# The first three tiles of a decoder layer side by side, and an account of the DMA wire in the planner

## The chip, the cores and the metric

The kernel runs on one core of one Trainium2 chip. The metric is the device time of one execution in microseconds (us); lower is better. TensorE multiplies matrices, VectorE (DVE) and ScalarE (ACT) work elementwise, GpSimd (POOL) fills and copies a little, and SP issues nearly all DMA transfers from one queue that it serves in order.

## The reference

One step of a decoder layer for a prompt of 256 tokens and 8 sequences of 8 new tokens: 320 rows of 2048 columns. One input projection feeds two token mixers (mLSTM, "ml", and HGRN2, "hg") and two merge gates; four more weight matrices follow.

```python
proj = jnp.einsum('btd,de->bte', x, w_in)
(ml_q, ml_k, ml_v, ml_i, ml_f, ml_o, hg_q, hg_f, hg_i, hg_g, gate_a, gate_b) = jnp.split(proj, offs, axis=-1)
h, C, n, m = _mlstm(q, k, v, ig, lf, C0, n0, m0)         # ig, lf from ml_i, ml_f
branch_a = norm(h) * jax.nn.sigmoid(ml_o)
o, S = _hgrn2(hq, jnp.log(f), 1.0 - f, hi, S0)           # f from hg_f
branch_b = rms(o) * jax.nn.silu(hg_g)
merged = jax.nn.sigmoid(gate_a) * (branch_a @ w_branch_a) + jax.nn.sigmoid(gate_b) * (branch_b @ w_branch_b)
x1 = _layernorm(DEEPNORM_ALPHA * x + merged @ w_out, ln1_g, ln1_b)
y = _layernorm(DEEPNORM_ALPHA * x1 + jnp.square(jax.nn.relu(x1 @ w_up)) @ w_down, ln2_g, ln2_b)
```

The outputs are y and the new states of both mixers. The mixers' states of the 8 sequences (C0: 4 heads, S0: 8 heads) are read from memory, updated and written back. All inputs are float32.

## The kernel before

**Main stream.** The six matrix products are cut into 304 tiles of 128 output columns (`tile_list`, `TILES`). A tile sums 16 k-steps of 128 rows into one PSUM bank. The tokens are the moving operand (320 columns), the weights the stationary one. Each float32 operand is split into a high half, rounded to the fast format fp32r (`xh`, `wh`), and the rest (`xl`, `wl`); a k-step is three products, high by high, high weight by low x, low weight by high x. So a tile is 48 products.

**Units.** Weights arrive as half tiles of 8 k-steps (`UNITS`, 512 KB each), in three raw buffers (`wr`, `RAW`). `prep` makes a unit's high half on ACT and its low half on VectorE, into one of three pairs of buffers (`wh`, `wl`, `HL`; five more from `bb` late in the kernel), and then plans the transfer of the unit three places on (`reload`) into the raw buffer just freed. The first six units are the first halves of tiles 0, 1, 2 and then their second halves (`FIRST` is 3).

**The start.** `start` issues the first transfers: unit 0 in three pieces from ACT's queue; x in pieces (k-steps 0, 1, 2 and 3, 4 to 7, 8 to 11, 12 to 15) from SP's queue, with units 1 and 2 between them; then the eight columns of the mLSTM gates (`wif`, in pieces of 32 bytes into a zeroed buffer `gw`), vectors and constants. Nine products of ones are issued on TensorE ahead of the real ones. `first` splits x and unit 0 piece by piece. After 24 k-steps, the first halves of tiles 0 to 2, `gates` multiplies x with `gw` in 16 small products of full float32; `rows` then computes the gate rows of the mLSTM (two products with `cst`, a chain of VectorE and ACT work, six transposes) and writes them to memory, from where each head reads them.

**Side work.** While the main stream runs, the evictions of the tiles and the mixers' work run beside it as Python generators ("chains"). A planner (`Sched`) writes the order of every engine by hand: it holds an assumed time for each engine and steps every chain that can go on, after each k-step of the main stream (`pump`). A chain's TensorE work is put into the order when its assumed operands are older than the assumed time of TensorE, and at most 0.9 us of it after each k-step. ACT and VectorE take a step that is assumed ready within 0.3 us if the engine is at most 0.9 us ahead. SP takes any that is ready within 0.3 us. A transfer is assumed landed a constant time after its issue (`+ 3200.0` for a unit, `+ 3500.0` for a part of C, `+ 4500.0` for S, `later(2500)` for an output). The times decide nothing but the order: on the chip, semaphores wait for what is really there, and every engine works off its order in sequence.

The input projection's side work lies in the first 850 us: 4 mLSTM heads, each with 16 parts of C loaded, used, updated and stored (256 KB each way, 14 buffers), then 8 HGRN2 heads with two groups of S each. From then on it is evictions and two layer norms; at the end a last part makes the prompt's new states and writes y.

Of the kernel before, what the change touches and what calls it, by code (L numbers as in the profile page):

```python
# [74 lines left out]
UNITS = [(i, half) for half in range(2) for i in range(FIRST)] + [(i, half) for i in range(FIRST, len(TILES)) for half in range(2)]  # L75
# [67 lines left out]
class Sched:  # L143
    PE_SIDE = 900.0

    def __init__(self):
        self.t = dict(pe=0.0, act=0.0, dve=0.0, pool=0.0, sp=0.0)
        self.chains = []
        self.pe_left = 0.0

# [7 lines left out]
    def use(self, eng, ready, cost):  # L158
        start = max(self.t[eng], ready)
        self.t[eng] = start + cost  # L160
        return start + cost

    def step(self, c, now):
# [27 lines left out]
        else:  # L191
# [18 lines left out]
            c.ready, c.eng, c.send = end, kind, end  # L210
        c.req = None
# [82 lines left out]
class Program:  # L294
# [43 lines left out]
    def dma(self, out, in_):  # L338
        self.nc.sync.dma_start(out, in_)  # L339

# [141 lines left out]
    def reload(self, u, at):  # L482
        t = yield ("sp", 620, lambda: self.dma(self.wr[:, u % self.RAW, :], self.d["wt"][u]), (at,))
        self.raw_at[u] = t + 3200.0

    def run_main(self):
        s = self.s
        todo = {}
        for n in range(len(TILES) * KT):
# [4 lines left out]
            if n == 0:  # L494
                self.first()
            elif n == 8 * FIRST:
                self.gates()
            if k == 0:
                self.before(i, t)
                s.until(lambda: self.mbank.free)  # L500
                self.mbank.free.sort(key=lambda x: x[0])
                at, b = self.mbank.free.pop(0)
                mh, ml, evs = self.moving(t)
                todo[i] = b, b[:, :mh.shape[2]], mh, ml, evs
                s.t["pe"] = max(s.t["pe"], at)
            b, o, mh, ml, evs = todo[i]
            if n < 8 * (FIRST + 1):
                s.t["pe"] = max(s.t["pe"], self.x_at[k], self.w_at[k] if u == 0 else 0.0)
# [20 lines left out]
        s.until(lambda: not s.chains)  # L529

# [79 lines left out]
    def start(self):  # L610
        nc, s, d = self.nc, self.s, self.d
        self.carve()
        P1 = self.Part(self.f1)
        xs, gw = P1.three(KT, TOK), P1.three(KT, 32)
# [6 lines left out]
        x = lambda lo, hi: self.dma(xs[:, lo:hi, :], d["xT"][:, lo:hi, :])  # L621
        for c in (slice(0, 256), slice(256, 512), slice(512, 1024)):
            nc.scalar.dma_start(self.wr[:, 0, c], d["wt"][0, :, c])
        nc.scalar.preload_act_table_set("natural_log_exp_and_others")
        x(0, 1)
        x(1, 2)
        x(2, 4)
        x(4, 8)
        self.dma(self.wr[:, 1, :], d["wt"][1])
        x(8, 12)  # L630
        self.dma(self.wr[:, 2, :], d["wt"][2])
        x(12, 16)
        nc.gpsimd.memset(gw, 0.0)
        self.dma(gw[:, :, 0:8], d["wif"])
        for u, at in ((1, 9000.0), (2, 12000.0)):
            self.raw_at[u] = at
        self.dma(self.vec, d["vec"])
        self.dma(self.cst, d["cst"])
# [9 lines left out]
        self.hl_free = [(0.0, (self.wh[:, i, :], self.wl[:, i, :])) for i in range(self.HL)]  # L648
        self.xs, self.gw = xs, gw
        for e in s.t:  # L650
            s.t[e] = 2000.0
        self.rows_ev, self.load_ev = Ev(), Ev()
# [20 lines left out]
    def first(self):  # L673

        s, v = self.s, self.nc.vector
        self.x_at, self.w_at = [0.0] * KT, [0.0] * 8
        hi, lo = self.hl_free.pop(0)[1]
        raw = self.wr[:, 0, :]
        f = lambda x: x.bitcast(F32)

# [7 lines left out]
        def x(a, b, at):  # L688
            c = slice(a, b)
            self.x_at[a:b] = [halves(self.xs[:, c, :], self.xh[:, c, :], self.xl[:, c, :], TOK * (b - a), at)] * (b - a)  # L690

        def w(a, b, at):
            c = slice(128 * a, 128 * b)
            self.w_at[a:b] = [halves(raw[:, c], hi[:, c], lo[:, c], 128 * (b - a), at)] * (b - a)

        x(0, 1, 3100.0)
        w(0, 2, 3500.0)
        x(1, 2, 3900.0)
# [1333 lines left out]
```

## Time and profile before

| | us |
|---|---|
| three timed runs | 2328.22, 2330.11, 2330.88 |
| their median | 2330.11 |
| the profiled execution's own time | 2327.19 |
| its span on the core | 2325.1 |
| TensorE busy in it | 2312.7 |
| VectorE, ACT busy | 1346.9, 1055.1 |

A timeline row gives start and length in us, engine, line of the kernel, operation, output<-inputs, shapes and a count; in brackets stands the idle time before it and what ended it. PE is TensorE, PEld its weight loads, SPq and ACTq are the engines' queues that issue transfers. A matmul's length overlaps the next one's, so the pace is the distance between starts. A windows row gives a stretch, its length, then each engine's busy time and number of instructions, the granted TensorE clock (PEclk, 1.00 is full), the busy share of the DMA engines and GB/s. A row of transfers gives count, size and the median time from issue to landing. A wait row gives who waited for whom: total us, times, longest.

### The profile page before, as it was taken

The numbers are of one execution on the slowest core, as the hardware profiler recorded it, in microseconds if no ns is written. First come the engines' busy times: TensorE is split into PE (matmuls) and PEld (weight loads), VectorE is DVE, ScalarE is ACT, GpSimd is POOL, SyncE is SP. The second block draws the span as 40 slices with busy tenths as digits, with TensorE's granted clock in tenths as the row PEclk, the third lists the DMA queues.
The fourth block names the chain that finished last, engine by engine and source line by source line (L and its number), as shares of the span: only waits on it lengthen the run. The fifth ranks groups of instructions, "written<-read, shape, count | busy, mean of one in ns | idle before, by whom it ended". The sixth has DMA issues, their size and how long they took to land.

```text
span 2325.1 us, 38931 instructions
## 1 busy us (share of the span) xinstructions
PE 2312.7 (99%) x15808; PEld 2270.0 (98%) x15808; DVE 1346.9 (58%) x2279; ACT 1055.1 (45%) x1685; POOL 11.5 (0%) x36
## 2 busy tenths in 40 slices
PE   9999999999999999999999999999999999999998
PEld 8999999999999999999999999999999999999997
DVE  5565566667676776555555767654444444444455
ACT  4444445455556665444433446542443343334333
POOL 0000000000000000000000000000000000000000
PEclk9999999999999999999999999999999999999999
DMA  7576858665555555555555644444444444444465
GB/s 247 195 258 204 291 187 281 224 215 173 196 181 188 182 185 172 177 174 172 176 171 174 215 166 154 147 152 146 154 146 154 146 154 147 153 148 152 149 221 183
DMA packets 145626, 424.91 MB, mean 183 GB/s; under 512 B 18468, under 2 KB 39972, under 8 KB 144424
## 3 DMA queue, kind: packets, MB, share of 16 engines
q1 hardware_dynamic: 143864, 415.63, 53.3%
q0 software_dynamic: 1152, 6.29, 0.8%
q8 instruction: 123, 2.02, 0.3%
q10 hardware_dynamic: 432, 0.52, 0.1%
q14 instruction: 55, 0.45, 0.1%
HBM read 371.48 MB, written 50.90 MB: 182 GB/s over the span
## 4 chain that ended last, share of the span: by engine, by line
PE 98%; ACT 1%; DMA 1%; SPq 0%; DVE 0%; issue 0%; ACTq 0%; DVEq 0%
PE bank L336 96%; DMA wr<-wt 1%; SPq L339 0%; ACT f3m L330 0%; PE bank L1158 0%; PE bank L929 0%; PE bank L1593 0%; PE bank L1431 0%; DVE f3m L1921 0%; ACT f L330 0%; PE bank L1485 0%; PE bank L1436 0%; PE bank L1002 0%; PE bank L976 0%; PE bank L1542 0%
## 5 line engine op out<-in xcount | busy, mean ns | idle before, releaser
L336 PE MATMUL bank<-xh,wh 128*128 128x320 f32 (+1 forms) x2432 | 785.6, 323 | 1.0 <-ACT xh L330 0.8
L475 DVE TENSOR_TENSOR wl<-wr,wh 128x1024 fp32r<-128x1024 f32 x431 | 528.0, 1225 | 423.1 <-ACT wh L330 419.0
L336 PE MATMUL bank<-xh,wl 128*128 128x320 f32 (+1 forms) x2432 | 754.5, 310 | 0.0
L336 PE MATMUL bank<-xl,wh 128*128 128x320 f32 (+1 forms) x2432 | 752.6, 309 | 1.3 <-DVE xl L685 1.3
L330 ACT ACTIVATE wh<-wr 128x1024 fp32r<-128x1024 f32 (+1 forms) x434 | 457.4, 1054 | 504.1 <-PE bank L336 486.1
L336 PEld LDWEIGHTS bank<-xh,wh 128*128 128x128 f32 x2432 | 459.0, 189 | 20.4 <-issue 15.0
L336 PEld LDWEIGHTS bank<-xl,wh 128*128 128x128 f32 x2432 | 459.4, 189 | 4.8 <-DVE xl L685 1.9
L336 PEld LDWEIGHTS bank<-xh,wl 128*128 128x128 f32 x2432 | 459.2, 189 | 0.1
L475 DVE TENSOR_TENSOR bb<-wr,bb 128x1024 fp32r<-128x1024 f32 x176 | 215.6, 1225 | 228.7 <-ACT bb L330 228.5
L330 ACT ACTIVATE bb<-wr 128x1024 fp32r<-128x1024 f32 x176 | 186.4, 1059 | 312.0 <-PE bank L336 292.8
L336 PE MATMUL bank<-xh,bb 128*128 128x320 f32 (+1 forms) x1280 | 285.4, 309 | 0.0
L336 PE MATMUL bank<-rxb,bb 128*128 128x320 f32 x1208 | 276.3, 309 | 0.0
L336 PE MATMUL bank<-ra,wh 128*128 128x320 f32 x988 | 265.9, 309 | 0.0
L336 PE MATMUL bank<-ra,bb 128*128 128x320 f32 x1096 | 264.3, 309 | 0.7 <-DVE ra L1623 0.7
L336 PEld LDWEIGHTS bank<-xh,bb 128*128 128x128 f32 x1280 | 215.0, 188 | 0.0
L336 PEld LDWEIGHTS bank<-rxb,bb 128*128 128x128 f32 x1208 | 204.5, 188 | 0.2
L336 PE MATMUL bank<-xl,bb 128*128 128x320 f32 (+1 forms) x640 | 197.7, 309 | 0.0
L336 PEld LDWEIGHTS bank<-ra,bb 128*128 128x128 f32 x1096 | 187.1, 188 | 1.2 <-DVE ra L1623 0.9
L336 PEld LDWEIGHTS bank<-ra,wh 128*128 128x128 f32 x988 | 176.3, 188 | 0.0
L336 PE MATMUL bank<-rxb,wh 128*128 128x320 f32 x548 | 169.0, 308 | 0.0
L336 PE MATMUL bank<-rxb,wl 128*128 128x320 f32 x548 | 169.0, 308 | 0.0
L336 PEld LDWEIGHTS bank<-xl,bb 128*128 128x128 f32 x640 | 120.4, 188 | 0.3 <-DVE xl L1846 0.3
(261 smaller groups left out, 2213.7 us busy)
## 6 DMA issues: line engine op xcount, KB each, us to landing
wr<-wt SPq DMA_DIRECT2D x607, 512.0 KB, 3.3
rx<-C SPq DMA_DIRECT2D x34, 256.0 KB, 5.2
Cs<-rx SPq DMA_DIRECT2D x34, 256.0 KB, 5.0
f<-C SPq DMA_DIRECT2D x30, 256.0 KB, 4.7
Cs<-f SPq DMA_DIRECT2D x30, 256.0 KB, 4.6
vD<-ra SPq DMA_DIRECT2D x4, 1024.0 KB, 9.0
f<-S SPq DMA_DIRECT2D x8, 512.0 KB, 6.1
f3h<-S SPq DMA_DIRECT2D x8, 512.0 KB, 6.6
```

Source lines behind the costliest of these rows:

```text
L330: return self.nc.scalar.activation(out, in_, func, **kw)
L336: self.nc.tensor.matmul(*a, **kw)
L475: self.V().tensor_tensor(lo, raw, hi.bitcast(F32), ALU.subtract)
```

## The change

**The first three tiles** leave `UNITS`. A new input `first` holds, for every k-step, x (320 columns) and the three tiles' weights (3 x 128) side by side (`STEP`, 704 columns). `start` loads it into `f1` and `f3`: k-step 0 as weights from ACT's queue and x from SP's, then k-steps 1, 2, 3 alone and the others in pairs from SP's. Then come the gates' columns, now contiguous and spread into `gw` by a POOL copy, vectors, and the first three units (of tiles 3 and 4). `lead` takes the place of `first`: it splits each k-step's x and weights on ACT and VectorE and issues the nine products of the k-step into three banks, by kind of product over the three tiles in the first four k-steps and tile by tile from then on. The weights' halves use `wh` and `wl` as eight slots of 384 columns. After the last k-step the evictions of the three tiles are put into the order, then the preparation of two units, then the gates' products.

**The planner** keeps a time for the DMA wire. A transfer is assumed to begin 1.5 us after its issue or when the wire is free, to take its bytes at 380 bytes per ns, and to land 0.6 us later; this landing replaces the constants. SP takes a step only if it is at most 0.9 us ahead, and not before the eighth transfer back is assumed landed. This holds for all transfers planned after the start.

```diff
-UNITS = [(i, half) for half in range(2) for i in range(FIRST)] + [(i, half) for i in range(FIRST, len(TILES)) for half in range(2)]
+UNITS = [(i, half) for i in range(FIRST, len(TILES)) for half in range(2)]
+STEP = TOK + 128 * FIRST
...
+    def transfer(self, at, size):
+        self.wire = max(at + 1500.0, self.wire) + size / 380.0
+        self.lands.append(self.wire + 600.0)
...
+            elif kind == "sp":
+                if r > now + 300 or self.t[kind] > now + 900:
+                    return False
+                r = max(r, self.lands[-8])
             elif r > now + 300:
                 return False
             end = self.use(kind, r, cost)
             fn()
             c.ready, c.eng, c.send = end, kind, end
+            if kind == "sp":
+                c.send = self.lands[-1]
...
     def dma(self, out, in_):
         self.nc.sync.dma_start(out, in_)
+        self.s.transfer(self.s.t["sp"], 4 * math.prod(out.shape))
...
-        self.raw_at[u] = t + 3200.0
+        self.raw_at[u] = t
...
-        for c in (slice(0, 256), slice(256, 512), slice(512, 1024)):
-            nc.scalar.dma_start(self.wr[:, 0, c], d["wt"][0, :, c])
+        first = d["first"]
+        nc.scalar.dma_start(self.xw[0][:, TOK:STEP], first[:, 0, TOK:STEP])
         nc.scalar.preload_act_table_set("natural_log_exp_and_others")
...
+        self.dma(self.xw[0][:, 0:TOK], first[:, 0, 0:TOK])
+        for lo, hi in ((1, 2), (2, 3), (3, 4), (4, 6), (6, 8), (8, 10), (10, 12)):
+            self.dma(raw[0][:, lo:hi, :], first[:, lo:hi, :])
+        for lo in (0, 2):
+            self.dma(raw[1][:, lo:lo + 2, :], first[:, 12 + lo:14 + lo, :])
         nc.gpsimd.memset(gw, 0.0)
-        self.dma(gw[:, :, 0:8], d["wif"])
+        self.dma(wif, d["wif"])
+        nc.gpsimd.tensor_copy(gw[:, :, 0:8], wif.rearrange("p (k n) -> p k n", n=8))
         self.dma(self.vec, d["vec"])
+        for u in range(self.RAW):
+            self.dma(self.wr[:, u, :], d["wt"][u])
+            self.raw_at[u] = 19000.0 + 1500.0 * u
...
+        pe = 4700.0
+        for k in range(KT):
+            at = 3400.0 + 950.0 * k
+            c = slice(384 * (k % 8), 384 * (k % 8) + 384)
+            xh, xl = self.xh[:, k, :], self.xl[:, k, :]
+            halves(self.xw[k][:, 0:TOK], xh, xl, TOK, at)
+            pe = max(pe, halves(self.xw[k][:, TOK:STEP], wh[:, c], wl[:, c], 384, at))
+            hi, lo = wh[:, c], wl[:, c]
+            jobs = [(i, w, x) for i in range(FIRST) for w, x in ((hi, xh), (hi, xl), (lo, xh))]
+            if k < 4:
+                jobs = [jobs[3 * i + j] for j in range(3) for i in range(FIRST)]
+            for n, (i, w, x) in enumerate(jobs):
+                self.mm(bank[i][:, :TOK], w[:, 128 * i:128 * i + 128], x, start=k == 0 and w is hi and x is xh, stop=k == KT - 1 and w is lo)
+                if k == KT - 1 and n % 3 == 2:
+                    s.t["pe"] = pe + 147.0 * (n + 1)
+                    s.spawn(self.evac(TILES[i], bank[i]), 0)
+            pe += 147.0 * 3 * FIRST
+            for i, last in enumerate((10, 13, 15)):
+                if k == last:
+                    self.hl_free.append((pe, (self.wh[:, i, :], self.wl[:, i, :])))
+        s.t["pe"] = pe + 300.0
+        s.pump(s.t["pe"])
+        s.t["pe"] = pe
         self.prep(True)
-        x(8, 12, 11000.0)
         self.prep(True)
-        x(12, 16, 13500.0)
...
-            self.mm(b[32 * x:32 * x + 32, :TOK], self.gw[:, k, :], self.xs[:, k, :], start=k < 4, stop=k >= KT - 4)
-        s.t["pe"] += 2500.0
+            self.mm(b[32 * x:32 * x + 32, :TOK], self.gw[:, k, :], self.xw[k][:, 0:TOK], start=k < 4, stop=k >= KT - 4)
+        s.t["pe"] += 2200.0
         s.spawn(self.rows(b), 1)
         s.spawn(self.lb(), 2)
+        s.pump(s.t["pe"])
...
-        m["bc_"].t = t + 3000.0
+        m["bc_"].t = t
...
-    def later(self, dt):
+    def later(self):
         e = Ev()
-        e.t = self.s.t["sp"] + dt
+        e.t = self.s.lands[-1]
         return e
...
-            m["parts"][n].t = t + 3500.0
+            m["parts"][n].t = t
...
-        m["ld"].t = t
+        m["ld"].t = self.s.t["sp"]
         m["sat"] = Ev()
-        m["sat"].t = t + 4500.0
+        m["sat"].t = t
```

More of the change, by code (lines that the diff above doesn't have):

```diff
@@ L529, in run_main, with take @@
         s.until(lambda: not s.chains)
+    def take(self):
+        s = self.s
+        s.until(lambda: self.mbank.free)
+        self.mbank.free.sort(key=lambda x: x[0])
+        at, b = self.mbank.free.pop(0)
+        s.t["pe"] = max(s.t["pe"], at)
+        return b
     def give(self, u):
@@ L814, in rows @@
         self.scr = scr
[L815 removed]
+        self.scr_at = t0
     def m_start(self, h):
```

99 lines of the change are left out of this document (35 added, 64 removed).

## The prediction

> **What bounds the kernel now.** I read the page first: busy shares, then the chain that ended last.
>
> ```profile
> span 2325.1 us, 38931 instructions
> PE 2312.7 (99%) x15808; PEld 2270.0 (98%) x15808; DVE 1346.9 (58%) x2279; ACT 1055.1 (45%) x1685; POOL 11.5 (0%) x36
> PE 98%; ACT 1%; DMA 1%; SPq 0%; DVE 0%; issue 0%; ACTq 0%; DVEq 0%
> ```
>
> TensorE is the bound, and a change can win only where it waits or runs slow. The windows view, cut at the places that matter, says where that is.
>
> ```profile
> core 0: us, PE busy (x) PEld busy (x) DVE busy (x) ACT busy (x) POOL busy (x), PEclk, DMA share, GB/s
> 4.99:8.41 3.42, 2.11 (x8) 1.15 (x7) 2.26 (x5) 2.31 (x6) 0.00 (x0) 1.00 1.03 406
> 8.41:15.23 6.82, 5.80 (x20) 5.40 (x21) 5.86 (x6) 5.30 (x5) 0.00 (x0) 0.50 0.96 314
> 15.23:21.98 6.75, 6.75 (x48) 6.56 (x46) 1.62 (x2) 1.19 (x2) 0.40 (x1) 1.00 0.94 314
> 21.98:24.27 2.29, 2.29 (x34) 0.94 (x33) 1.54 (x2) 1.68 (x3) 0.00 (x0) 1.00 0.13 48
> 24.27:36.87 12.60, 12.42 (x81) 10.89 (x77) 6.86 (x15) 5.29 (x11) 0.20 (x1) 1.00 0.51 166
> 36.87:100.00 63.13, 63.13 (x439) 60.85 (x438) 38.49 (x73) 28.58 (x44) 0.00 (x0) 1.00 0.68 236
> 100.00:850.00 750.00, 750.00 (x5236) 718.46 (x5235) 495.26 (x1111) 397.14 (x795) 4.66 (x13) 1.00 0.63 212
> 850.00:2298.00 1448.00, 1447.34 (x9858) 1446.33 (x9857) 776.84 (x1026) 596.49 (x790) 4.38 (x8) 1.00 0.49 163
> 2298.00:2325.00 27.00, 18.91 (x84) 15.47 (x83) 18.17 (x44) 15.47 (x31) 0.00 (x0) 0.89 0.60 222
> ```
>
> From 36.87 to 2298 us the idle time is 0.66 us in all: the second half of the change, which touches those 2261 us, finds nothing to win there in waits. In 850:2298, 9858 products took 1448 us, so one product at full clock is 0.1469 us. The loss is at the start, and the timeline shows its parts.
>
> ```profile
> 0.73 1.39 ACTq L623 DMA_DIRECT2D wr<-wt  x3
> 0.74 1.82 SPq L339 DMA_DIRECT2D f<-xT  x4
> 0.99 4.17 PE L336 MATMUL bank<-ones 128*128 128x128 f32 x18 [0.99 <-POOL ones L616]
> 4.59 0.47 ACT L330 ACTIVATE xh<-f 128x320 fp32r<-128x320 f32 x1 [1.16 <-DMA f<-xT]
> 4.97 0.40 ACT L330 ACTIVATE wh<-wr 128x256 fp32r<-128x256 f32 x1
> 5.09 0.49 DVE L685 TENSOR_TENSOR xl<-f,xh 128x320 fp32r<-128x320 f32 x1 [5.09 <-ACT xh L330]
> 5.27 0.47 ACT L330 ACTIVATE xh<-f 128x320 fp32r<-128x320 f32 x1
> 5.42 0.41 PE L336 MATMUL bank<-xh,wh 128*128 128x320 f32 x1 [0.26 <-ACT wh L330]
> 5.50 0.42 DVE L685 TENSOR_TENSOR wl<-wr,wh 128x256 fp32r<-128x256 f32 x1
> 5.84 0.49 DVE L685 TENSOR_TENSOR xl<-f,xh 128x320 fp32r<-128x320 f32 x1
> 6.63 0.32 PE L336 MATMUL bank<-xh,wl 128*128 128x320 f32 x1
> 7.74 0.41 PE L336 MATMUL bank<-xh,wh 128*128 128x320 f32 x1 [0.79 <-ACT xh L330]
> 8.59 0.63 PE L336 MATMUL bank<-xl,wh 128*128 128x320 f32 x1 [0.45 <-DVE xl L685]
> 11.40 0.64 PE L336 MATMUL bank<-xl,wh 128*128 128x320 f32 x1 [0.84 <-DVE xl L685]
> 21.98 2.36 PE L336 MATMUL bank<-f 128*32 128x320 f32 x32
> 27.37 0.70 PE L336 MATMUL bank<-f,cst 128*4 128x320 f32 x2 [0.18 <-ACT f L330]
> 36.87 0.30 PE L336 MATMUL bank<-xh,wh 128*128 128x320 f32 x1
> ```
>
> The first half units of tiles 0 to 2 are 72 products: 5.42 to 21.98, 16.56 us against 72 x 0.1469 = 10.58. The 5.98 us are waits for pieces of x (7.74, 8.59, 11.40) and a granted clock of 0.50 from 8.41 to 15.23, which the idle stretches brought on. Then come the gates' products (21.98), the second halves, and at 36.87 the first product of tile 3.
>
> **The change, part by part.** (a) *Loads.* A k-step now brings x (160 KB) and three weight pieces (192 KB) at once, and feeds nine products, 1.32 us, where a k-step of x fed three, 0.44 us. What was hungry is the first pass: it needed all of x (2.5 MB) and half the weights within 10.6 us. Now the pass takes 144 x 0.1469 = 21.15 us and needs 5.77 MB. The wire, one number per us from 0:
>
> ```profile
> GB/s 0 22 204 251 338 390 420 394 417 430 398 424 405 155 66 117 364 298 287 365 410 303 94 16 29 299 287 221 254 385 99 0 33 254 238 0 0 90 352 94
> ```
>
> From 5 to 13 us it moves 410 GB/s, so 0.36 MB every 0.88 us: ahead of TensorE. x's first 160 KB were on the wire together with the ACT queue's 128 KB (0.3 MB moved at about 3.4 us) and were used at 4.59, 1.2 us later. By the same sums k-step 1 (0.72 MB moved) is usable at 5.9, 2 at 6.9, 3 at 7.8, 4 at 9.6, 6 at 11.3, 14 at 18.3.
>
> (b) *Splitting.* ACT's starts are 0.38 us apart after 320 columns (4.59, 4.97) and 0.30 after 256 (4.97, 5.27), so about 0.46 after 384: 0.84 a k-step. VectorE: 0.41 (5.09, 5.50) and 0.34 (5.50, 5.84), so 0.48 and 0.89. Both stay below TensorE's 1.32, so TensorE becomes the pace. The first weight piece is wider by 128 columns: its ACT copy takes about 0.54 instead of 0.40, so the first product starts near 5.56 instead of 5.42, 0.14 later. TensorE then asks for k-step 1 at about 6.9 (split from 5.9, high half ready 6.8), 2 at 8.3, 3 at 9.6, 4 at 10.9, 6 at 13.6: all there. The first six products of before start about 0.24 apart (5.42 to 6.63); for the same unsteadiness I allow 0.3. The pass ends at 5.56 + 21.15 + 0.3 = 27.0.
>
> (c) *Evictions, then preparation, then gates.* On ACT the three evictions now stand ahead of the high halves of tile 3's first unit, so these wait for the end of the pass. From like rows:
>
> ```profile
> 37.07 0.44 ACT L330 ACTIVATE f<-bank 128x320 f32<-128x320 f32 x1 [1.78 <-PE bank L336]
> 37.40 0.45 ACT L330 ACTIVATE f<-f 4x320 f32<-4x320 f32 x1
> ```
>
> and the page's groups of the same copy and subtraction:
>
> ```profile
> L330 ACT ACTIVATE wh<-wr 128x1024 fp32r<-128x1024 f32 (+1 forms) x434 | 457.4, 1054 | 504.1 <-PE bank L336 486.1
> L475 DVE TENSOR_TENSOR wl<-wr,wh 128x1024 fp32r<-128x1024 f32 x431 | 528.0, 1225 | 423.1 <-ACT wh L330 419.0
> ```
>
> An eviction occupies ACT 0.33 us; the last starts 0.2 after the pass's end, the unit's high half follows at +0.5 and lasts 1.05, its low half 1.23, so it is there at +2.85. The gates' 32 products cover 2.39 of that (2.29, and an allowance of 0.1 for the change of operands), the next two products 0.4: 0.1 is left as a wait. If the gates' cover were gone, it would be 2.4. The second unit is ready at about +4.1 and wanted at +5.9. The next reload can start at +2.9 and is wanted three units (10.6 us) later.
>
> (d) *POOL and the queues.* The gates' columns now arrive in one contiguous transfer and are spread by one POOL copy (at most the 0.40 us POOL is busy in 15.23:21.98, for twice the columns); it waits for a transfer behind 5.8 MB, about 18 us, and POOL's memsets queue behind it, first wanted after 27. SP moves the first three units (1.5 MB, 3.8 us at 410 GB/s) behind x: there at about 22.5, wanted at 27. ACT issues one transfer instead of three (1.39 us at 0.73); its gain is covered by the 1.16 us in which ACT waits for x. All nothing.
>
> (e) *Row products.* 24.27:36.87 holds 72 products (10.58) and 2.02 of row products with their 0.18 wait (27.37 is the first pair). They come after tile 3's start now, at the same cost.
>
> (f) *The account of the wire* changes only in which order work is issued. It replaces constants after the issue: a unit's reload 3.2 becomes 1.5 + 1.38 + 0.6 = 3.48 on an idle wire, a C part 3.5 becomes 2.79, and more behind other transfers. Measured from the issue:
>
> ```profile
> wr<-wt SPq DMA_DIRECT2D x607, 512.0 KB, 3.3
> rx<-C SPq DMA_DIRECT2D x34, 256.0 KB, 5.2
> ```
>
> and SP's own waits:
>
> ```profile
> SPq L339 <- DVE wl L475: 879.5, 307, 15.0
> ```
>
> For C the account errs toward too early by 0.71 more than the constant did. If each of the 8 C groups and 8 S groups then stood 0.71 too early in TensorE's order, that is 11.4 us lost; at the other end nothing, since TensorE shows no wait for them. I take 0, the value that 100:850 shows under the old constants. Side products may also fall into other places. A return from a transpose to the main stream:
>
> ```profile
> 45.24 0.39 PE L336 MATMUL bank<-xh,wh 128*128 128x320 f32 x1
> 45.47 0.31 PE L336 MATMUL bank<-xl,wh 128*128 128x320 f32 x1
> ```
>
> 0.23 instead of 0.147, so 0.08 a return; 15 places more or fewer are 1.2 us, either sign. I take 0.
>
> *Sum.* Before: tile 3 at 36.87, less the row products 2.02: 34.85. After: 27.0 + 2.39 + 0.1 = 29.5. The gain is 5.3 us, all at the start. Of the profiled execution, 2327.19 us (span 2325.1), that leaves 2321.9. The three timed runs are 2328.22 to 2330.88, median 2330.11, 2.9 above the profiled one; by the median it is 2324.8. I see only the start's clock stretches as a cause for such a spread (the granted clock changed after 3.42 and again after 6.82, twice 3.41; 3.41 us at half clock cost 1.7), and a pass without idle time should meet fewer, so I go between: 2323.5.
>
> *A rule against a row.* In 4.99:8.41 TensorE was busy 2.11 of 3.42 us, and the clock halved after it; in the first half of 8.41:15.23 it stood idle 0.84 us before 11.40 and the clock stayed low. So partly busy stretches cost the clock here. The Trainium skill (TensorE: Matmul & The Clock Gate, What's actually happening) has the array go to half rate after at least one idle window of about 3.4 us, and back after a busy one. By that no stretch after the change would be slowed; the trace does not bear the first half out, and the sum by the row is the first rival.
>
> **The rivals.** *1. The clock still halves.* After the change the stretch 4.99:8.41 has about 2.7 to 3.0 busy us of 3.42: between the 2.11 that lost the clock and a full one. One such stretch costs 1.7: 2325.2; two, 2326.9. Against it: x and weights are there, so a slowed TensorE is full and recovers. 0.20.
>
> *2. Late weights: slower.* SP now refuses a transfer when it is more than 0.9 us ahead, reloads among them, and an assumed landing moves by up to eight transfers. If in the crowded loads of C a reload falls behind and its unit is late, TensorE waits a unit's ACT and VectorE time, 1.05 + 1.23 = 2.3 us. One in each of the 8 C groups: 18.4, so 2342. From the fifth it is slower by over 0.2% (5.3 + 4.7 = 10.0). For it: SP spends 879.5 us waiting for buffers of the units, and what stands behind waits too. Against: three buffers give 10.6 us, the turn needs 1.05 + 1.23 + 3.3 = 5.6, and the wire is 63% busy. 0.10.
>
> *3. The gain is given back* in side products (1.2), some early C groups (0.71 each) and the end: 2298:2325 is bound by ACT, VectorE and output transfers, whose order the account may change. Some 4 us: 2327.5. 0.12.
>
> *4. The pieces do not overlap.* Sixteen k-steps in eleven transfers, each taking its whole time from issue to landing, at the least the 3.85 us from 0.74 to 4.59: 42 us, so the pass ends some 16 us later than I say: 2339. The wire's row, 390 to 430 GB/s with pieces of 128 to 640 KB, speaks against it. 0.02. The Trainium skill (DMA: Bandwidth & Descriptors, Measured) advises transfers of 1 MiB or more for 75% of peak and would count against pieces of 352 KB; this trace does not agree while several are queued.
>
> **How the numbers follow.** Forecast 0.56, with its own range 2320 to 2326.5 (1.2 for side products, 2 for the clock). A measurement here tells about 0.2%, 4.7 us: faster means below 2325.4, slower above 2334.8. Faster: most of the forecast and a third of rival 1, 0.58. Same: the rest of rival 1, rival 3 and the forecast's edge, 0.30. Slower: rivals 2 and 4, 0.12. The range runs from 2319 (the profiled execution's sum less 1.2 and one clock stretch) to 2330 (rival 3 with a clock stretch), and leaves out rivals 2 and 4 and a little below.
>
> **What would show it.** First product near 5.6; no wait over 0.3 us on TensorE until the gates' products near 27; clock 1.00 from 5 us on (rival 1: a 0.50 stretch); tile 3 near 29.5. ACT and VectorE a step ahead throughout the pass. No idle time on TensorE from 37 to 2298 us and no wait on a wr transfer (rival 2). The end still 27 us long. I am wrong if x or weights arrive later than the wire's row says, if C or S products wait, or if the number of returns changes by dozens.

## The result

Before and after were timed in turn on one chip, seven runs each. Before has a median of 2329.77 us (2328.22 to 2332.29), after 2321.28 us (2320.65 to 2321.49). The ratio is 0.9962, with a 95% interval of 0.9951 to 0.9974: 8.5 us less. The profiled execution of after took 2321.41 us (span 2319.6), 5.8 us less than that of before. The forecast was 2321.9 for the profiled execution and 2323.5 for the median.

The page of after begins:

```profile
span 2319.6 us, 38982 instructions
PE 2309.1 (100%) x15808; PEld 2267.0 (98%) x15808; DVE 1351.6 (58%) x2297; ACT 1059.5 (46%) x1703; POOL 11.9 (1%) x37
PE 98%; ACT 1%; DVE 0%; DMA 0%; issue 0%; SPq 0%; ACTq 0%; DVEq 0%
```

Still 15808 products and nearly the same busy time; the 1% of the chain that lay on DMA is gone. The stretches of after, in the same columns as those of before:

```profile
4.86:8.41 3.55, 3.22 (x22) 2.95 (x22) 2.25 (x6) 2.12 (x5) 0.00 (x0) 1.00 1.02 367
8.41:15.23 6.82, 6.82 (x47) 6.56 (x46) 6.08 (x15) 5.77 (x15) 0.00 (x0) 1.00 1.01 411
...
29.42:872.69 843.27, 843.27 (x5874) 807.63 (x5871) 560.30 (x1224) 446.23 (x871) 4.68 (x13) 1.00 0.64 213
```

Between 8.41 and 15.23, where before ran 20 products at half clock, 47 products run at full clock. The timeline of after shows the places that the prediction spoke of:

```profile
3.93 0.47 ACT L342 ACTIVATE xh<-f 128x320 fp32r<-128x320 f32 x1 [1.47 <-DMA f<-first]
4.86 0.71 PE L348 MATMUL bank<-xh,wh 128*128 128x320 f32 x3
7.17 0.47 ACT L342 ACTIVATE xh<-f 128x320 fp32r<-128x320 f32 x1 [1.33 <-DMA f<-first]
8.10 0.71 PE L348 MATMUL bank<-xh,wh 128*128 128x320 f32 x3 [0.33 <-ACT wh L342]
18.83 0.42 POOL L646 COPY f<-f 128x128 f32<-128x128 f32 x1 [17.42 <-DMA f<-wif]
27.13 1.82 PE L348 MATMUL bank<-f,f 128*32 128x320 f32 x24
27.57 2.00 ACT L342 ACTIVATE wh<-wr 128x1024 fp32r<-128x1024 f32 x2
29.42 0.42 PE L348 MATMUL bank<-xh,wh 128*128 128x320 f32 x1
29.68 0.31 PE L348 MATMUL bank<-xl,wh 128*128 128x320 f32 x1
29.93 0.41 PE L348 MATMUL bank<-xh,wl 128*128 128x320 f32 x1
```

The first product starts at 4.86, the gates' at 27.13, tile 3 at 29.42; in before these stood at 5.42, 21.98 and 36.87, with 2.02 us of row products ahead of tile 3 that after has behind it. Of TensorE's waits after the start only those for a k-step's weights (0.33 us, at 8.10) and for the last part of the kernel (0.7 us) are left.

To compare all kernels I cut the span at two products of the main stream, counted in the traces: the first of tile 3 and the first of tile 103, 4800 main products later, behind the mixers' last side work. Before's row for the stretch between them:

```profile
36.87:878.46 841.59, 841.59 (x5868) 807.75 (x5867) 553.09 (x1211) 442.27 (x865) 4.66 (x13) 1.00 0.63 213
```

That is 841.59 us against 843.27, and 843.27 less the 2.02 us of row products is 841.25: nothing is lost or won there, between these two executions. (One group of C takes 0.6 us longer in this execution of after than in e_after's below.) The rest of the span is 1446.63 us in before and 1446.94 in after. So the 5.5 us by which the spans differ are the start: 36.87 - 2.02 - 29.42 = 5.43.

### The profile page after: what moved, and what is told of

It is laid out like the page before. It is cut to its first block, busy times and chain, and to the rows that moved or that the text cites. A ratio compares the mean times of both kernels' runs of the same rounds, so it can differ in the third digit from the quotient of the medians.

```text
span 2319.6 us, 38982 instructions
## 1 busy us (share of the span) xinstructions
PE 2309.1 (100%) x15808; PEld 2267.0 (98%) x15808; DVE 1351.6 (58%) x2297; ACT 1059.5 (46%) x1703; POOL 11.9 (1%) x37
## 3 DMA queue, kind: packets, MB, share of 16 engines
q8 instruction: 123, 2.02, 0.4%
## 4 chain that ended last, share of the span: by engine, by line
PE 98%; ACT 1%; DVE 0%; DMA 0%; issue 0%; SPq 0%; ACTq 0%; DVEq 0%
PE bank L348 97%; ACT f3m L342 0%; DMA f<-first 0%; PE bank L1610 0%; PE bank L946 0%; PE bank L1175 0%; PE bank L1448 0%; DVE f3m L1938 0%; ACT f L342 0%; PE bank L1453 0%; PE bank L1019 0%; PE bank L1502 0%; PE bank L993 0%; PE bank L1559 0%; ACT oC L342 0%
## 5 line engine op out<-in xcount | busy, mean ns | idle before, releaser
L488 DVE TENSOR_TENSOR wl<-wr,wh 128x1024 fp32r<-128x1024 f32 x426 | 522.0, 1225 | 399.6 <-ACT wh L342 395.9
L342 ACT ACTIVATE wh<-wr 128x1024 fp32r<-128x1024 f32 x426 | 451.0, 1059 | 498.1 <-PE bank L348 478.2
```

Source lines behind the costliest of these rows:

```text
L342: return self.nc.scalar.activation(out, in_, func, **kw)
L488: self.V().tensor_tensor(lo, raw, hi.bitcast(F32), ALU.subtract)
```

## The experiments

In the profiled executions of all kernels (us):

| | tile 3 starts | tile 3 to tile 103 | tile 103 to the end | execution |
|---|---|---|---|---|
| before | 36.87 | 841.59 | 1446.63 | 2327.19 |
| e_before | 38.89 | 842.54 | 1446.53 | 2329.75 |
| e_fill | 35.98 | 841.99 | 1446.55 | 2326.47 |
| e_account | 37.84 | 841.51 | 1446.47 | 2327.93 |
| e_lead | 29.56 | 850.51 | 1446.22 | 2328.46 |
| e_lead_c | 29.66 | 847.76 | 1446.71 | 2326.23 |
| e_lead_s | 29.03 | 852.91 | 1446.76 | 2330.56 |
| e_queue | 29.33 | 844.85 | 1446.29 | 2322.70 |
| e_landings | 29.84 | 842.87 | 1447.06 | 2321.56 |
| e_after | 29.58 | 842.79 | 1446.82 | 2320.95 |
| after | 29.42 | 843.27 | 1446.94 | 2321.41 |
| e_pieces | 29.84 | 842.86 | 1446.59 | 2321.36 |
| e_two_queues | 29.48 | 842.67 | 1447.08 | 2321.01 |
| e_late_evict | 29.52 | 842.60 | 1446.92 | 2320.84 |

The last column differs from the start times and stretches by the 2 us around the span. Each ratio below is against before, timed in the same batch on the same chip. Rows with the new start hold 2.02 us of row products in the second column that the others do not.

### What the old start costs: e_before and e_fill

The prediction's median rested on a guess: that before's executions differ by stretches of halved clock at the start. e_before is before, unchanged. e_fill keeps TensorE busy in the first pass with products of ones into a bank that the gates' products overwrite later:

```diff
             kk = slice(128 * (k % 8), 128 * (k % 8) + 128)
+            self.fill({2: 4}.get(n, 0))
             self.mm(o, hi[:, kk], mh[:, k, :], start=k == 0, stop=False)
+            self.fill({2: 2, 4: 8}.get(n, 0))
             self.mm(o, hi[:, kk], ml[:, k, :], start=False, stop=False)
...
+    def fill(self, count):
+        for _ in range(count):
+            self.mm(self.gbank[:, 0:128], self.ones, self.ones, start=True, stop=True)
```

> The kernel before, unchanged, to see the granted clock of each timed execution. Theory A (the 3 us by which the profiled execution lies below the median of the kernel before are half-clock stretches at the start, which fall differently from run to run): the mean clock differs from execution to execution, lower where the time is longer, and each 1.7 us of time goes with about 0.0015 in the mean clock (3.41 us at half clock out of 2325); times spread over 3 us or more. Rival B (the spread has nothing to do with the clock): the mean clock is 0.997 in all of them.

Measured: median 2329.16 us (2327.60 to 2332.01, 11 runs), ratio 1.0001 (0.9993 to 1.0010). Its profile caught a slower execution than the one in the prediction: 2.0 us more at the start, 1.0 us more in the mixers' stretch. At the start k-steps 2 and 3 of x were late. From the timeline of before, then from the timeline and the windows of e_before:

```profile
6.94 0.74 ACT L330 ACTIVATE xh<-f 128x640 fp32r<-128x640 f32 x1 [0.90 <-DMA f<-xT]
```

```profile
8.53 0.74 ACT L330 ACTIVATE xh<-f 128x640 fp32r<-128x640 f32 x1 [2.39 <-DMA f<-xT]
9.32 0.64 PE L336 MATMUL bank<-xh,wh 128*128 128x320 f32 x1 [2.34 <-ACT xh L330]
```

```profile
8.53:18.70 10.17, 8.54 (x29) 7.79 (x30) 8.18 (x7) 7.19 (x7) 0.00 (x0) 0.50 0.84 271
```

The same piece, issued in the same place, was used 1.6 us later, TensorE stood idle 2.34 us instead of 0.79, and the clock was at half for 10.2 us instead of 6.8. The mean granted clocks, which the expectation was about, decide nothing: the three longest executions (2331.13 to 2332.01) have 0.997, but so has the shortest (2327.60). Nor could they: 3.41 us at half clock lower a mean over 2325 us by 0.0007, half of what the expectation says, and the means are given to 0.001.

> The kernel before with 14 products of ones put into TensorE's order in the waits of its first pass (4 ahead of k-step 2, 2 inside it, 8 inside k-step 4), so that TensorE has work while x arrives and is split. Same transfers, same splits. Theory A (the clock is part of the loss, the supply of x the rest): no stretch at 0.50 after 5 us; the wait for the low half of x's k-steps 4 to 7 stays, until about 11.4, after it 59 products at 0.147 end near 20.1, so the gates start at 20.1 to 20.5 instead of 21.98; the median is 1.7 to 5 us below the kernel before, and the times spread less than 1.5 us. Rival B (idle time alone matters): gates start at 21.5 or later, median within 1 us of before, the spread as before.

Measured: median 2329.55 us (2326.47 to 2332.38, 11 runs), ratio 1.0002 (0.9993 to 1.0011). The windows of e_fill:

```profile
8.40:15.20 6.80, 5.77 (x44) 5.51 (x43) 5.59 (x5) 5.69 (x6) 0.00 (x0) 1.00 0.97 323
```

With the clock kept at 1.00 from 8.4 us on, the pass ended 0.9 us earlier in the profile (gates at 21.10 instead of 21.98), and not more, because the pass then waits for x. The median did not move, so neither theory fits in full: the gates start where neither put them, and the median goes with rival B. The executions of e_fill lie 5.9 us apart, and nine of the eleven, all with a mean granted clock of 0.999, lie from 2326.47 to 2332.16. So halved clock at the start is, as far as these means tell, not what sets the executions apart, and filling it is worth at most 1.6 us (the interval's lower end). What the pass then lacks is x.

### One half of the change at a time: e_account and e_lead

e_account is before with the account of the wire and nothing of the new start. Its core:

```diff
+    def transfer(self, at, size):
+        self.wire = max(at + 1500.0, self.wire) + size / 380.0
+        self.lands.append(self.wire + 600.0)
...
+            elif kind == "sp":
+                if r > now + 300 or self.t[kind] > now + 900:
+                    return False
+                r = max(r, self.lands[-8])
...
-        self.raw_at[u] = t + 3200.0
+        self.raw_at[u] = t
...
+        s.wire, s.lands = 15000.0, [15000.0] * 8
...
-            m["parts"][n].t = t + 3500.0
+            m["parts"][n].t = t
```

> The kernel before with the planner's account of the wire alone; the start is the old one. Theory A (all of the gain is in the start): start and end as before, TensorE idle between 37 and 2298 us under 1 us, median within 1.5 us of before. Rival B (the account wins part of the 8.5 us between the medians, or lets the start win it): 2 us or more below before. Rival C (the account costs and the start wins more than is seen): 2 us or more above before.

Measured: median 2327.93 us (2326.85 to 2328.65, 11 runs), ratio 0.9994 (0.9985 to 1.0003). In its profile TensorE ran at half pace until 17.4 us; the timeline of e_account shows the step from products 0.27 apart, as under the granted clock of 0.50 in before, to 0.15:

```profile
17.06 0.47 PE L347 MATMUL bank<-xh,wl 128*128 128x320 f32 x1
17.33 0.35 PE L347 MATMUL bank<-xh,wh 128*128 128x320 f32 x1
17.52 0.31 PE L347 MATMUL bank<-xl,wh 128*128 128x320 f32 x1
```

The column of the granted clock does not show this half clock. A window of e_account has 1.00 with 21 products in 5.40 us:

```profile
12.00:17.40 5.40, 5.40 (x21) 5.40 (x22) 4.79 (x4) 3.42 (x3) 0.00 (x0) 1.00 0.82 218
```

So at the start of an execution a 1.00 in that column is no proof of full clock, and the distance between products has to be read beside it.

Its mixers' stretch took 841.51 us, as before's 841.59. With the old start the account is worth 1.4 us by the ratio (0.0006 x 2329), and the interval reaches no change. Its 11 executions lie only 1.8 us apart.

e_lead is the other half: after, with the account and SP's two tests taken out and the old constants put back. Its core:

```diff
-            elif kind == "sp":
-                if r > now + 300 or self.t[kind] > now + 900:
-                    return False
-                r = max(r, self.lands[-8])
...
-        self.raw_at[u] = t
+        self.raw_at[u] = t + 3200.0
...
-        e.t = self.s.lands[-1]
+        e.t = self.s.t["sp"] + dt
...
-            m["parts"][n].t = t
+            m["parts"][n].t = t + 3500.0
```

> The changed kernel with the planner's old constants: the first three tiles side by side alone. Theory A: 2321.3 within 1 us, first product near 4.9, tile 3 near 29.4, clock 1.00 from 5 us on. Rival B (the account carries part of the gain): 2323.5 or more. Rival C (the account costs): 2319.5 or less.

Measured: median 2326.43 us (2325.35 to 2328.46, 11 runs), ratio 0.9990 (0.9981 to 0.9998): 2.3 us of gain, where the new start by itself should bring 5.4. Tile 3 starts at 29.56, so the gain is made; it is given back later. The windows of e_lead hold the mixers' stretch and two places in it, and the timeline of its TensorE the first of the two:

```profile
29.56:880.07 850.51, 846.88 (x5874) 808.45 (x5871) 557.40 (x1224) 444.64 (x871) 4.73 (x13) 1.00 0.63 211
286.16:292.69 6.53, 4.17 (x19) 0.71 (x18) 3.06 (x9) 1.37 (x4) 0.00 (x0) 1.00 0.84 289
341.81:346.68 4.87, 3.60 (x19) 0.71 (x17) 3.47 (x6) 2.78 (x5) 0.00 (x0) 1.00 0.87 334
```

```profile
286.16 0.31 PE L342 MATMUL bank<-xh,wl 128*128 128x320 f32 x1
...
286.87 1.44 PE L342 MATMUL bank<-f 128*32 128x512 f32 x6
289.64 1.04 PE L342 MATMUL bank<-f 128*32 128x512 f32 x2 [1.33 <-DMA f<-C]
291.71 1.04 PE L342 MATMUL bank<-f 128*32 128x512 f32 x2 [1.03 <-DMA f<-C]
292.69 0.41 PE L342 MATMUL bank<-xh,wh 128*128 128x320 f32 x1
```

A group of C is 16 products in a row between two main products, and the main products around it stand 2.09 us apart when nothing is late, as here in the timeline of after:

```profile
272.82 0.30 PE L348 MATMUL bank<-xh,wl 128*128 128x320 f32 x1
...
273.52 1.46 PE L348 MATMUL bank<-f 128*32 128x512 f32 x10
274.91 0.42 PE L348 MATMUL bank<-xh,wh 128*128 128x320 f32 x1
```

In e_lead two of the eight groups take 6.53 and 4.87 us: 4.44 + 2.78 = 7.22 us more than 2 x 2.09, and the whole stretch is 7.24 us longer than after's. The loss is these two groups, which TensorE's order has ahead of the landing of their parts: theory A's median of 2321.3 failed, and rival B's 2323.5 or more came true. (This is the slowest of e_lead's executions; the median lies 2.0 us lower.) SP's queue shows why those landed late. From e_lead's timeline of SP, and its waits from 280 to 286.5 us and, ahead of the second group, from 325 to 346 us:

```profile
280.33 0.84 SPq L345 DMA_DIRECT2D wr<-wt  x1
285.77 0.34 SPq L345 DMA_DIRECT2D f<-C  x1
```

```profile
SPq L345 <- DMA Cs<-f: 4.5, 1, 4.5
```

```profile
SPq L345 <- DMA Cs<-rx: 7.5, 4, 2.7
```

Ahead of the first group SP stood 4.5 us at a load of C into a buffer whose store had not landed, with the next loads and reloads behind it; ahead of the second it stood 7.5 us in four such waits. The constant of `m_store` assumes that a store has landed 2.5 us after its issue; the page of after has 4.4 and 4.8 us:

```profile
Cs<-rx SPq DMA_DIRECT2D x34, 256.0 KB, 4.4
Cs<-f SPq DMA_DIRECT2D x30, 256.0 KB, 4.8
```

So start alone 2.3 us, account alone 1.4, both 8.9 (0.0038 x 2329): some 5 us come only from the two together.

### Which part of the account: e_landings, e_queue, e_after

e_landings is after without SP's two tests, so that the account only gives the assumed landings. e_queue is e_lead with the two tests and the account behind them, but with the old constants as landings. e_after is after, unchanged.

```diff
# e_landings, against after
-            elif kind == "sp":
-                if r > now + 300 or self.t[kind] > now + 900:
-                    return False
-                r = max(r, self.lands[-8])
# e_queue, against e_lead
+            elif kind == "sp":
+                if r > now + 300 or self.t[kind] > now + 900:
+                    return False
+                r = max(r, self.lands[-8])
```

> The changed kernel without the two tests on SP's queue (at most 0.9 us ahead, eighth transfer back landed): landings by the account of the wire, issue as before. Theory A (the assumed landings are what counts): within 1 us of the changed kernel, no wait for C. Rival B (the tests on the queue count): 3 us or more above the changed kernel, waits for C or for weights.

> The new start with the old constants for landings, and the two tests on SP's queue (the account of the wire is kept only for the eighth transfer back). Theory A (landings count): waits for C stay in the profile, median 2325 or more. Rival B (the queue's order counts): no waits for C, median within 1 us of the changed kernel.

> The changed kernel, unchanged, on the same chip as the three others, as their reference. All theories: ratio 0.996 to the kernel before, executions within 1.5 us of each other, mean clock 0.999 in each.

Measured: e_landings 2321.47 us (2321.16 to 2321.67, 5 runs), ratio 0.9965 (0.9952 to 0.9977); e_queue 2322.70 us (2321.89 to 2323.76, 7 runs), ratio 0.9970 (0.9960 to 0.9981); e_after 2320.89 us (2320.22 to 2321.31, 5 runs), ratio 0.9962 (0.9948 to 0.9976). The landings alone give all of it (0.6 us short of e_after, inside the intervals). The tests alone give nearly all, 1.8 us short, which lies between the two theories for e_queue: one group of C still takes 2.93 us, and its stretch is 844.85 us. The two late groups of e_lead are gone either way. SP's waits for stores of C are not what tells them apart. The waits of SP between 36 and 850 us, of before and then of e_queue:

```profile
SPq L339 <- DMA Cs<-f: 24.0, 15, 4.0
SPq L339 <- DMA Cs<-rx: 23.2, 17, 3.7
```

```profile
SPq L349 <- DMA Cs<-f: 31.9, 18, 5.4
SPq L349 <- DMA Cs<-rx: 27.6, 17, 4.5
```

e_queue waits 59.5 us there and before 47.2, with little or no loss on TensorE (after waits 27.0); so what counts would be whether a group of C stands behind such a wait at the wrong moment. That is inferred from these waits and not tried by itself.

### One constant at a time: e_lead_c and e_lead_s

If two groups come too early under the constants, a longer constant should do what the account does. e_lead_c takes C's parts as landed after 5500 ns, e_lead_s the stores of C.

```diff
# e_lead_c, against e_lead
-            m["parts"][n].t = t + 3500.0
+            m["parts"][n].t = t + 5500.0
# e_lead_s, against e_lead: m_store
-        yield wait(self.later(2500))
+        yield wait(self.later(4500))
```

> The new start with the old constants, in which TensorE waited for parts of C (1.3, 1.3 and 1.1 us as idle time, some 4 us between starts), and one constant longer: a part of C is assumed landed 5.5 us after its issue instead of 3.5. Theory A (the constant for C was too early for the transfers' real 4.5 to 5.4 us, and the earlier start only brought it out): no wait for C in the profile, median 4 us below the new start with old constants (about 2322.5). Rival B (what the account wins is the order on SP's queue): waits for C go but others take their place, or the median stays above 2325.

> The new start with the old constants, and one constant longer: the store of a part of C is assumed landed 4.5 us after its issue instead of 2.5, so its buffer is given to the next load later in SP's order. Theory A (SP stands before a load until the store of its buffer has landed, 47 us in the mixers' stretch of the kernel before, 62 us with the new start and old constants, 25 us with the account; what stands behind comes late and TensorE meets it): SP's waits for stores fall below 40 us, tile 3 to product 4944 takes 842.5 to 845 us instead of 850.5, median 2321 to 2323.5. Rival B (it is the sum of all the constants, or chance of alignment): waits fall but the stretch stays above 846, median above 2324.5.

Measured: e_lead_c 2326.23 us (2325.19 to 2326.94, 11 runs), ratio 0.9983 (0.9974 to 0.9992); e_lead_s 2331.59 us (2330.56 to 2332.41, 11 runs), ratio 1.0010 (1.0002 to 1.0019), slower than before in spite of the new start. In both theory A failed (it had 2322.5, and 2321 to 2323.5). Neither shows a wait of TensorE for a part of C any more, and in e_lead_s SP's waits for stores of C fall to 22.4 us. Yet the mixers' stretch is 4.5 and 9.6 us longer than after's, and most of that lies in one other place (idle time of TensorE alone: 2.40 and 6.05 us). The windows between the last main product ahead of head 3's first tile and that tile's first, of e_lead_c and of e_lead_s:

```profile
254.51:263.89 9.38, 6.98 (x48) 3.85 (x46) 7.46 (x21) 4.65 (x13) 0.00 (x0) 1.00 1.00 362
```

```profile
253.00:269.01 16.01, 9.96 (x55) 5.82 (x53) 11.08 (x34) 5.81 (x16) 0.00 (x0) 0.79 0.92 316
```

No main product stands in 9.38 and 16.01 us: the order has 44 and 51 side products there in a row. This is written into the order. As the code has it, `before` holds the main stream at a head's first tile until the buffers of an earlier head are planned to be free (`s.until(lambda: self.vr.free and self.qk.free)`), and with every part or every buffer 2 us later in the plan, that work is not done by then. (This is read from the code and the order; it wasn't tried by itself.) The dependent steps then run one after the other on TensorE, VectorE and ACT with no main product beside them, and TensorE waits for VectorE, longest in this row of e_lead_s's timeline:

```profile
256.83 1.07 PE L939 MATMUL bank<-cst,f 128*128 128x128 f32 x4 [2.53 <-DVE f L1226]
```

After this wait the clock was at half for 6.8 us. A window of e_lead_s:

```profile
256.90:263.70 6.80, 4.85 (x17) 3.08 (x21) 5.07 (x15) 1.09 (x4) 0.00 (x0) 0.50 0.96 335
```

So with SP's queue unchecked each set of constants tried under the new start lost on one side: short, and a group of C meets its parts too early; one of them long, and a head isn't planned to be done when the next one needs its buffers. The short constants are not wrong by themselves, since e_queue keeps them and loses little. The account gives a short landing when the wire is free and a long one when it is not, and after shows neither loss.

### The pieces of the new start: e_pieces, e_two_queues, e_late_evict

Three edits of after. e_pieces loads k-steps 1 to 3 and then four at a time. e_two_queues issues k-step 2 from ACT's queue. e_late_evict leaves out the stop in which the planner puts the evictions ahead of the preparation of the two units.

```diff
# e_pieces
-        for lo, hi in ((1, 2), (2, 3), (3, 4), (4, 6), (6, 8), (8, 10), (10, 12)):
+        for lo, hi in ((1, 4), (4, 8), (8, 12)):
             self.dma(raw[0][:, lo:hi, :], first[:, lo:hi, :])
-        for lo in (0, 2):
-            self.dma(raw[1][:, lo:lo + 2, :], first[:, 12 + lo:14 + lo, :])
+        self.dma(raw[1], first[:, 12:16, :])
# e_two_queues
+        nc.scalar.dma_start(self.xw[2], first[:, 2, :])
...
-        for lo, hi in ((1, 2), (2, 3), (3, 4), (4, 6), (6, 8), (8, 10), (10, 12)):
+        for lo, hi in ((1, 2), (3, 4), (4, 6), (6, 8), (8, 10), (10, 12)):
# e_late_evict
-        s.t["pe"] = pe + 300.0
-        s.pump(s.t["pe"])
```

> The changed kernel with the lead's transfers in larger pieces: k-steps 1 to 3, 4 to 7, 8 to 11, 12 to 15, four transfers instead of nine after k-step 0. Theory A (the pass lives from landing of each piece; small ones first): k-step 1 lands with k-step 3, near 7.2 to 8, so TensorE waits about 1.5 us at 6.2 and about 1 more for k-steps 4 to 7; tile 3 2 us later, median 1.5 to 3 above the changed kernel; the clock may halve after the wait, since 2.1 busy of 3.42 us did it in the kernel before (then 3.5 to 5 above). Rival B (larger pieces move faster): within 0.5 us of the changed kernel.

> The changed kernel with k-step 2 on ACT's queue behind k-step 0's weights, so that SP's queue has one transfer less ahead of k-step 3. Theory A (k-step 2 is late because it is third in one queue): the 0.64 us at k-step 2 and the 0.3 at k-step 4 shrink, tile 3 0.3 to 0.7 earlier, median 0.3 to 0.7 below the changed kernel. Rival B (the two queues share the wire and k-step 1 gets what k-step 2 wins): the wait moves to k-step 1, median within 0.3 us or above.

> The changed kernel with the evictions of the first three tiles behind the preparation of the two units in ACT's order. Theory A (the gates' products cover either order): tile 3 starts within 0.3 us, median within 0.5 us of the changed kernel. Rival B (the order matters): the low half of tile 3's first unit is ready 2 us earlier and the start gains, or the bank of tile 3 is late and it loses, by 0.5 us or more.

Measured, five runs each: e_pieces 2321.29 us (2321.04 to 2321.66), e_two_queues 2320.60 (2320.30 to 2321.23), e_late_evict 2320.55 (2320.33 to 2321.07); the ratios are 0.9964, 0.9962 and 0.9962, after's own 0.9962. None differs from after by anything that these runs can tell, so theory A failed for e_pieces (1.5 to 3 us) and for e_two_queues (0.3 to 0.7 us). In e_pieces TensorE waited for the second transfer, and tile 3 came 0.3 us later than in e_after, 29.84 to 29.58. The wait need not be the pieces': e_landings, with the same start as after, has 0.88 us at k-step 2 and tile 3 at 29.84 too. From TensorE's timeline of e_pieces:

```profile
7.40 0.71 PE L348 MATMUL bank<-xh,wh 128*128 128x320 f32 x3 [1.10 <-ACT wh L342]
```

In e_two_queues no wait was left in the first pass, but by the distance between products this execution began it at half clock. e_after, with nothing changed, shows the same two things, so neither need be the second queue's doing. TensorE's timeline of e_two_queues:

```profile
4.89 1.17 PE L348 MATMUL bank<-xh,wh 128*128 128x320 f32 x3
...
6.64 0.61 PE L348 MATMUL bank<-xh,wl 128*128 128x320 f32 x3
7.09 0.60 PE L348 MATMUL bank<-xh,wh 128*128 128x320 f32 x3
```

Six products took 1.75 us (4.89 to 6.64) where they later take 0.9, so tile 3 stood at 29.48, no earlier than in after. In e_late_evict tile 3 starts at 29.52: the evictions' place in the order is worth nothing that can be seen here.

## Why the prediction was right, point by point

**(a) Loads and (b) splitting** held. The waits that were left, 0.33 us at 8.10 and a step of 0.31 us instead of 0.15 at 11.30, stand where 0.3 us was allowed. They differ between executions of one kernel: e_after has no wait in the pass. The first product came at 4.86 instead of 5.56: x's first piece was used at 3.93, not 4.59. k-step 2 was used at 7.17, 0.3 us later than the sum over the wire's row. The pass ended at about 27.05, predicted 27.0: the 0.7 us won at the first product went into the waits and a pace of 0.150 us a product instead of 0.147 (126 products from 8.10). One sentence of (a) was wrong: the old first pass needed half of x, k-steps 0 to 7, and not all of it; the other half belongs to the second halves of the tiles. No term hung on it. In (c) the terms of the +2.85 add up to 2.78; nothing hung on that either.

**(c)** Tile 3 at 29.42, predicted 29.5. ACT began the unit's high half at 27.57, and its low half was used at 29.93, where the step from 29.68 is 0.25 instead of 0.15: the predicted 0.1 us of wait. e_late_evict agrees that the gates' products cover this part.

**(d)** POOL's copy ran at 18.83, and nothing waited for it. **(e)** The row products came behind tile 3 at the same cost: 843.27 - 2.02 against 841.59.

**(f)** "I take 0, the value that 100:850 shows under the old constants" is the step that failed. The sum was right, since after's mixers' stretch equals before's, but not for that reason: here the forecast was lucky. The constants showed no wait in before because its order, in that execution, had no group of C ahead of its parts. Under the new start they cost 7.2 us in e_lead's profile, more than the start gains, and 5.5 us between the medians (2326.43 and 2320.89; 6.5 by the ratios). So the new order of the mixers' work had a loss of some 6 us in it, and the account a gain of the same size; I had both at 0. The bound given, 11.4 us for sixteen groups 0.71 too early, was of that size, but with the wrong sign of the cause: the account was feared for a landing that is too early, and it was the constants, with nothing to hold SP back, that were.

**The sum.** 2321.9 for the profiled execution, 2321.41 measured.

**From the profile to the median**, the mis-sized term. Before's median stood 2.9 us above its profile, and I gave half of that back for clock stretches: 2323.5. After's median lies 0.1 us below its profile, so nothing of the 2.9 was left. The miss of 2.2 us is the 1.6 that I added to the sum, 0.5 in the sum and this 0.1. The cause given finds no support either: e_fill, with the clock full in its profile from 6.8 us on, has executions as far apart as before's. (Nor does the profile of before show a change of the clock at 4.99, where the 3.42 us begin: it has 1.00 from the start to 8.41.) What narrows them is seen over the four combinations:

| runs: lowest to highest | old constants | account |
|---|---|---|
| old start | e_before 4.4 us | e_account 1.8 us |
| new start | e_lead 3.1 us | e_after 1.1 us |

(11 runs each, 5 of e_after; after's own seven lie 0.8 us apart.) The account narrows it in both rows. For the new start alone 3.1 against 4.4 is too little to tell, and e_lead_c, under old constants but one, has 1.8 as well, so the account is not the only way. The profile of e_before shows one way for each: a late piece of x (2.0 us), and a group of C that took 3.21 us instead of 2.09. That is one execution, so how often each occurs stays open.

**The rivals.** Rival 1, the clock: it stayed at 1.00, with products at full pace, through the first pass of after, with 3.22 of 3.55 us busy in the first stretch. In e_after, the same kernel, the first six products took 1.76 us (from 5.02) instead of 0.9, which by that pace is half clock: so rival 1's clock does occur at the beginning, and tile 3 came only 0.2 us later, at 29.58. Rival 2, late weights: no TensorE wait on a unit's transfer. Rival 3, the gain given back: not in after, but it is what the new start does without the account (2327.5 forecast for it, 2326.43 measured in e_lead), by C groups alone. Rival 4, pieces that do not overlap: in 8.41:15.23 the wire moved 411 GB/s. The Trainium skill (DMA: Bandwidth & Descriptors, Measured) advises transfers of 1 MiB or more for 75% of peak; its table is of transfers issued from GpSimd. e_pieces, whose transfers are 1.1 and 1.4 MB instead of 0.35 and 0.7, moved 431 GB/s in 8.41:15.23 against 411 and was not faster (0.9964 against 0.9962), so for these transfers, queued one behind the other, the size was worth some 5% of the wire and nothing in the time.

**Not settled.** Which groups of C come early under which start is a matter of where the planner puts them; I did not derive it; that each edit of the planner moves them by chance is therefore not excluded for any one of these runs. The lowest median of any version, 2320.55 us in e_late_evict, lies 0.3 us below e_after's, less than the runs can tell.

## What to carry to other kernels

A stretch without waits shows that the order fits this alignment, not that the assumptions behind it are right: anything that moves the work ahead of it can bring the waits out, so a change to the start and a change to the planner have to be tried apart and together. Fixed latencies in the planner failed here in both directions once the order moved; give a planner the state of the wire, or look for late operands after each shift. And profile more than one execution before taking the difference between a profile and the median for something that a change will keep.

## What the runs showed of the hardware that I had not expected

- By the distance between products, the clock at the start differs between executions, of the same kernel too: full from the first product in after, half until about 6.8 us in e_after, 6.6 in e_two_queues and 17.4 in e_account, though TensorE there had products all the time from 9 to 10.4 and from 12 us on. The column of the granted clock has 1.00 in all four.
- A wait of 1.10 us between full stretches did not cost the clock (e_pieces); a wait of 2.53 us was followed by 6.8 us at half clock (e_lead_s, from 256.9). The Trainium skill (TensorE: Matmul & The Clock Gate, What's actually happening) names one idle window of about 3.4 us as the condition. If idle means without any work, the second case does not agree: the wait is shorter, and in the 3.41 us before the clock fell TensorE was busy for 0.81.
- Small pieces seem to hold a queue. In before SP's issue behind the gates' columns, 2048 pieces of 32 bytes, took 6.86 us; in after, with one contiguous transfer, the same issue took 0.33. (The transfers ahead of it differ too, and no run changes the pieces alone.) From the timeline of SP of before:

```profile
7.15 6.86 SPq L339 DMA_DIRECT2D vec<-vec  x1
```
